# First adaLN modulation of a diffusion trunk: a four-row product with split weights, or feature tiles with row sums on VectorE

## The chip, the cores and the metric

One core of one Trainium2 chip runs the whole program. The metric is the device time of one execution in microseconds (us), shown as the median of several runs.

## The reference, cut to what matters

Two layers work on 512 latent tokens and 256 context tokens of 1024 features. Ahead of each sub-layer the tokens are normalised, scaled and shifted; scale and shift come from the conditioning vectors `c` and `c_ctx` through `w_mod`. The change touches this for the first sub-layer of layer 0, and the product with the key and value columns of `w_in` that follows:

```
silu_c  = silu(c)                                   # (1, 1024); silu_cc likewise from c_ctx
sh1, sc1, g1, sh2, sc2, g2 = split(silu_c @ w_mod[0] + b_mod[0], 6)
h  = rmsnorm(x,  norm1_g[0]) * (1 + sc1)  + sh1     # 512 x 1024
hc = rmsnorm(xc, norm1_g[0]) * (1 + csc1) + csh1    # 256 x 1024
gk, gv = columns of h @ w_in[0] and hc @ w_in[0]    # 768 x 256
```

All inputs are fp32. Products of large size are made from parts: a value is split into `hi`, rounded to the matmul type fp32r, and `lo`, the rest, and three matmuls (hi hi, hi lo, lo hi) are summed.

## The kernel before, in words

Features lie on the 128 partitions, in eight tiles `k`; the 768 tokens are columns. Before layer 0 there is a start section (L407 to L499) in which the order of every engine and of the DMA queue on SP is written out by hand: the string `START` (L40) is a list of codes, each code calls a step, and each step appends its instructions to its engines' queues. The order of the codes is therefore the order in which each engine works, and an engine stops at the first instruction that waits.

The steps of the start section are these.

- `s` (L206) loads a piece of `w_mod`, 128 x 1024, into `sraw`. There are 16, four for each block of 512 output features; the four blocks are shift 0 to 511, scale 0 to 511, then the second halves.
- `e` and `E` (L211) split a piece into `shi` (ScalarE) and `slo` (VectorE for `e`, GpSimd for `E`). Nine of the 16 pieces are split.
- `t` (L219) multiplies a piece: the conditioning vectors are the stationary operand (4 columns), the weights stream through with 512 columns. A piece that was not split streams in fp32.
- `f` and `F` (L229, L233) copy the four rows of a finished block out, turn them onto partitions with four small matmuls, and write `mods` and, for scale, `scl1`.
- `x` (L412) loads a tile of the tokens (128 x 768), squares it and adds it to `acc`. `r` (L421) turns `acc` into `rb`, the reciprocal root for each token on all partitions: matmuls `ss`, `nv` on VectorE, the power `nr` on GpSimd, `dg` on VectorE, matmuls `nbc`, two copies.
- `d` and `p` (L435) multiply a token tile by `rb` on VectorE or GpSimd. `n` (L439) applies scale and shift and writes `hh`. `m` and `M` (L452) write `hl` on VectorE or GpSimd.
- `w` and `W` load and split the key and value weights. `g` (L457) makes the key and value product of four feature tiles: 6 token tiles x 3 matmuls each, into six PSUM tiles `kv0`. It is called with 0 and with 4, each time for four tiles.

After the codes, `silu_rows` (L467) makes `cb`, silu of both conditioning vectors spread over all partitions, with ScalarE and GpSimd. `cb` is what `mods_rest` (L248) needs later: it makes all other modulations as row sums on VectorE (L262), one `scalar_tensor_tensor` with an accumulator for each tile and vector.

The start section's pool is closed behind it. The tile `gt` (L586) lies in memory that the pool gave back, so its load waits until the last user of that memory is done. `rtab` (L596) needs `gt` and `rraw` (L588), and on VectorE it stands ahead of the value copies `gv` (L684), which free the PSUM tiles that the next product (L569) writes.

Of the kernel before, what the change touches and what calls it, by code (L numbers as in the profile page):

```python
# [88 lines left out]
def trunk(es: ExitStack, tc: tile.TileContext, xin, cvec, crow, vecs, gq, rope, wmod_s, wmod_t, w_in, w_gqa,  # L89
# [45 lines left out]

    cs4 = cp.tile([P, KT, 4], F32R, name="cs4")
    dve.tensor_copy(cs4[:, :, 0:2], cs)
    dve.tensor_sub(cs4[:, :, 2:4], cs, f32(cs4[:, :, 0:2]))
    cs0 = cp.tile([P, KT, 4], F32, name="cs0")
    dve.memset(cs0, 0.0)  # L140
    dve.tensor_copy(cs0[:, :, 0:2], cs)
    sel = cp.tile([4, 2], F32, name="sel")
    dve.tensor_add(sel, ident[0:4, 0:2], ident[0:4, 2:4])
# [58 lines left out]
    def mods_start(sp, blk):  # L202

        st = {}

        def load(kk):  # L206
            raw = sp.tile([P, 1024], F32, tag="sraw", bufs=6, name="sraw")
            dma.dma_start(raw, wmod_s[blk, kk])
            st[kk] = [(cs0, raw)]

        def split(kk, eng):  # L211
            raw = st[kk][0][1]
            hi = sp.tile([P, 1024], F32R, tag="shi", bufs=3, name="shi")
            lo = sp.tile([P, 1024], F32R, tag="slo", bufs=3, name="slo")
            act.copy(hi, raw)
            eng.tensor_sub(lo, raw, f32(hi))
            st[kk] = [(cs4, hi), (cs4, lo)]

        def mul(kk):  # L219
            if kk == 0:  # L220
                st["ps"] = psum("mm", "mps")
            for i in range(2):
                k = kk * 2 + i
                n = len(st[kk])
                for j, (c, w) in enumerate(st[kk]):
                    pe.matmul(st["ps"][0:4, :], c[:, k, :], w[:, i * 512:i * 512 + 512],
                              start=k + j == 0, stop=k == KT - 1 and j == n - 1)

        def row():  # L229
            st["row"] = sp.tile([4, 512], F32, tag="srow", bufs=2, name="srow")  # L230
            act.copy(st["row"], st["ps"][0:4, :])

        def fin():  # L233
            po = psum("t", "mpo")
            for i in range(4):
                pe.matmul(po[:, 2 * i:2 * i + 2], st["row"][:, i * P:i * P + P], sel, start=True, stop=True)
            f0 = blk * 4
            dve.tensor_tensor(mods[0][:, f0:f0 + 4, :], po[:, 0:8].rearrange("p (i v) -> p i v", v=2),
                              lv(0, V_BM + f0, 4).unsqueeze(2).broadcast_to([P, 4, 2]), ALU.add)
            if blk >= 2:  # L240
                f = f0 - 8
                for v in range(2):
                    dve.scalar_tensor_tensor(scl1[0][:, f:f + 4, v], mods[0][:, 8 + f:12 + f, v], 1.0,
                                             lv(0, V_N1 + f, 4), ALU.add, ALU.mult)

        return dict(s=load, e=lambda kk: split(kk, dve), E=lambda kk: split(kk, pool), t=mul, f=row, F=fin)
# [160 lines left out]
    with (tc.tile_pool(name="start", bufs=1) as sp,  # L407
# [49 lines left out]
        def kv_part(k0):  # L457

            for k in range(k0, k0 + 4):
                wh, wl = w2_first[k // 4]  # L460
                o = (k % 4) * 256
                for t, ps in enumerate(kv0):
                    for i, (a, w) in enumerate(((H[0][k], wh), (H[0][k], wl), (H[1][k], wh))):
                        pe.matmul(ps[:, :256], a[:, t * P:(t + 1) * P], w[:, o:o + 256],
                                  start=k + i == 0, stop=k == KT - 1 and i == 2)

        def silu_rows():  # L467

            raw = [mp.tile([P, D], F32, tag="mraw", bufs=2, name="crow") for _ in range(2)]
            th = [sp.tile([P, 1024], F32, tag="sraw", bufs=6, name="cth") for _ in range(2)]  # L470
            for v in range(2):
                dma.dma_start(raw[v], crow[v:v + 1, :].broadcast_to([P, D]))
                act.activation(th[v], raw[v], AF.Tanh, scale=0.5)
                pool.tensor_scalar(th[v], th[v], 0.5, 0.5, ALU.mult, ALU.add)
                pool.tensor_mul(cb[:, v, :], th[v], raw[v])

        for q in START.split():
            kind, i = q[0], int(q[1:])
            if kind == "w":
                w2_raw.append(raw_w(w_gqa[0, 2, i], 1024))  # L480
            elif kind == "W":
                w2_first.append(split_w(w2_raw[i], 1024))
            elif kind == "x":
                load_x(i)
            elif kind == "r":
                r_part(i)
            elif kind == "n":
                norm_part(i)
            elif kind in "mM":
                norm_low(i, dve if kind == "m" else pool)  # L490
            elif kind in "dp":
                xr_part(i, dve if kind == "d" else pool)
            elif kind in "fF":
                blks[i][kind]()
            elif kind == "g":
                kv_part(i)
            else:
                blks[i // 4][kind](i % 4)
# [1057 lines left out]
```

## Time and profile before

| what | us |
|---|---|
| median of 3 runs (2310.33 to 2311.14) | 2310.59 |
| the profiled execution | 2311.89 |
| its span, first to last instruction | 2310.1 |
| TensorE busy in the span | 2249.6 |
| VectorE busy | 1451.9 |
| ScalarE busy | 850.1 |
| GpSimd busy | 318.1 |

The profile is of one execution; 1.8 us lie outside its span. Busy time of TensorE counts matmuls from start to modelled end. "Releaser" is what ended an engine's wait. The granted clock of TensorE is given as a share of its upper level: 1.00 is 2.4 GHz and 0.50 is 1.2 GHz.

### The profile page before, as it was taken

How to read it: one execution, taken by the hardware profiler on the slowest of the kernel's cores; microseconds unless marked ns; L12 is line 12 of the kernel's file. 1: busy time of each engine (PE TensorE's matmuls, PEld its weight loads, DVE VectorE, ACT ScalarE, POOL GpSimd, SP SyncE). 2: the span in 40 equal slices, each digit the busy share in tenths (PEclk: the TensorE clock that was granted, in tenths of full speed). 3: DMA queues.
4: the chain of work that ended last, by engine and by line, in shares of the span. 5: the costliest groups of instructions: out<-in, count | busy, mean ns of one | idle time of the engine just before them, and what ended most of it. 6: DMA issues, size and time to landing. Idle time of an engine off the chain costs nothing.

```text
span 2310.1 us, 33414 instructions
## 1 busy us (share of the span) xinstructions
PE 2249.6 (97%) x12895; PEld 1953.2 (85%) x12895; DVE 1451.9 (63%) x2623; ACT 850.1 (37%) x1607; POOL 318.1 (14%) x308
## 2 busy tenths in 40 slices
PE   6899999999999999999999999999999999999998
PEld 2889888999888888888888888888888778888887
DVE  6596978877776366744532358978877655433334
ACT  5324555445621242112112234555445424322223
POOL 4301311112133020000000012311111221000000
PEclk9999999999999999999999999999999999999999
DMA  7432324444355324524521224233343553432322
GB/s 258 128 110 81 106 99 121 135 126 126 128 200 179 93 92 131 162 91 156 166 89 64 68 100 122 87 122 110 114 136 116 173 164 95 147 100 90 102 91 83
DMA packets 98463, 281.06 MB, mean 122 GB/s; under 512 B 12032, under 2 KB 19328, under 8 KB 98304
## 3 DMA queue, kind: packets, MB, share of 16 engines
q1 hardware_dynamic: 98304, 278.92, 38.1%
q8 instruction: 102, 1.67, 0.3%
q14 instruction: 57, 0.47, 0.1%
HBM read 228.15 MB, written 24.51 MB: 109 GB/s over the span
## 4 chain that ended last, share of the span: by engine, by line
PE 65%; DVE 2%; issue 1%; ACT 1%; DMA 0%; POOL 0%; SPq 0%; POOLq 0%; DVEq 0%; ACTq 0%
PE fg L190 13%; PE fu L190 13%; PE fo L190 13%; PE gt L190 6%; PE wo L190 5%; PE br L190 4%; PE o L1047 2%; PE gq L569 2%; PE s L970 2%; PE nv L190 1%; PE nk L190 1%; PE pt L1022 1%; PE nq L190 1%; PE ga L190 1%; PE va L190 1%
## 5 line engine op out<-in xcount | busy, mean ns | idle before, releaser
L172 ACT CAST whi<-wraw 128x1024 fp32r<-128x1024 f32 (+1 forms) x276 | 286.4, 1038 | 623.8 <-PE fo L190 181.8
L173 DVE TENSOR_TENSOR wlo<-wraw,whi 128x1024 fp32r<-128x1024 f32 (+1 forms) x276 | 343.0, 1243 | 215.6 <-ACT whi L172 210.1
L1004 POOL TENSOR_SCALAR pt<-pt,sm 128x768 f32<-128x768 f32 (+1 forms) x160 | 145.2, 907 | 761.8 <-DVE sm L1003 519.3
L752 DVE SCALAR_TENSOR_TENSOR y<-u,vec,y 128x783 f32<-128x783 f32 (+1 forms) x240 | 218.7, 911 | 1.5
L190 PE MATMUL gt<-hh,whi 128*128 128x512 f32 (+1 forms) x576 | 212.4, 369 | 0.0
L190 PE MATMUL gt<-hh,wlo 128*128 128x512 f32 (+1 forms) x576 | 204.8, 356 | 0.0
L190 PE MATMUL gt<-hl,whi 128*128 128x512 f32 (+1 forms) x576 | 204.7, 355 | 0.0
L190 PE MATMUL fo<-hidh,whi 128*128 128x512 f32 (+1 forms) x549 | 192.4, 350 | 0.0
L190 PE MATMUL fo<-hidh,wlo 128*128 128x512 f32 (+1 forms) x549 | 191.7, 349 | 0.0
L190 PE MATMUL fg<-hl,whi 128*128 128x512 f32 (+1 forms) x544 | 190.4, 350 | 1.1 <-POOL hl L342 0.9
L190 PE MATMUL fo<-hidl,whi 128*128 128x512 f32 (+1 forms) x549 | 191.5, 349 | 0.0
L190 PE MATMUL fg<-hh,whi 128*128 128x512 f32 (+1 forms) x544 | 190.3, 350 | 1.1 <-ACT hh L337 1.1
L190 PE MATMUL fg<-hh,wlo 128*128 128x512 f32 (+1 forms) x544 | 189.7, 349 | 0.0
L190 PE MATMUL fu<-hh,whi 128*128 128x512 f32 (+1 forms) x536 | 188.5, 352 | 0.6 <-ACT whi L172 0.6
L190 PE MATMUL fu<-hh,wlo 128*128 128x512 f32 (+1 forms) x536 | 188.3, 352 | 0.8 <-DVE wlo L173 0.8
L190 PE MATMUL fu<-hl,whi 128*128 128x512 f32 (+1 forms) x536 | 188.4, 352 | 0.0
L1024 ACT CAST pTh<-pt 128x384 fp32r<-128x384 f32 (+2 forms) x224 | 104.8, 497 | 136.9 <-PE pt L1022 136.1
L1025 DVE TENSOR_TENSOR pTl<-pt,pTh 128x384 fp32r<-128x384 f32 (+2 forms) x224 | 123.7, 568 | 19.5 <-ACT pTh L1024 18.3
L1365 DVE SCALAR_TENSOR_TENSOR xn<-fo,mods,xn 128x512 f32<-128x512 f32 (+1 forms) x75 | 48.2, 643 | 133.5 <-PE fo L190 133.5
L1348 DVE TENSOR_TENSOR sg<-fu,sg 128x512 f32<-128x512 f32 (+1 forms) x67 | 39.9, 595 | 137.8 <-PE fu L190 137.8
L190 PEld LDWEIGHTS gt<-hh,wlo 128*128 128x128 f32 x576 | 108.7, 189 | 16.3
L190 PEld LDWEIGHTS gt<-hh,whi 128*128 128x128 f32 x576 | 109.0, 189 | 11.1 <-ACT gtan L945 0.3
(264 smaller groups left out, 5449.1 us busy)
## 6 DMA issues: line engine op xcount, KB each, us to landing
wraw<-w_in SPq DMA_DIRECT2D x88, 512.0 KB, 3.5
wraw<-w_fi SPq DMA_DIRECT2D x88, 512.0 KB, 3.3
mraw<-wmod_t SPq DMA_DIRECT2D x80, 512.0 KB, 4.2
wraw<-w_fo SPq DMA_DIRECT2D x32, 448.0 KB, 3.4
gd<-gtan SPq DMA_DIRECT2D x48, 256.0 KB, 2.0
wraw<-w_br SPq DMA_DIRECT2D x24, 512.0 KB, 3.5
tg<-gd SPq DMA_DIRECT2D x24, 384.0 KB, 5.6
sraw<-wmod_s SPq DMA_DIRECT2D x16, 512.0 KB, 5.4
```

The costliest lines, as they stand in the source:

```text
L172: act.copy(hi[:, :n], raw[:, :n])
L173: last_lo[0] = dve.tensor_sub(lo[:, :n], raw[:, :n], f32(hi[:, :n])).ins
L190: pe.matmul(ps[:, :c1 - c0], w[:, k, :], a[k][:, c0:c1], start=i == 0, stop=i == 3 * n - 1)
L569: pe.matmul(ps[:, :256], a[k][:, t * P:(t + 1) * P], w[:, o:o + 256], start=i == 0, stop=i == 3 * KT - 1)
L752: dve.scalar_tensor_tensor(y[:, :YW], u[:, t:t + YW], w, y[:, :YW], ALU.mult, ALU.add)
L970: pe.matmul(o, Q[:, qc], k, start=i == 0, stop=i == 1)
L1004: pool.tensor_scalar(pt[:, :w], pt[:, :w], sm[:, 3:4], 1.0, ALU.mult, ALU.mult)
L1024: act.copy(hv[:, qi, k0:k0 + step, :], pv)
L1025: dve.tensor_tensor(lw[:, qi, k0:k0 + step, :], pv, f32(hv[:, qi, k0:k0 + step, :]), ALU.subtract)
L1047: pe.matmul(ops[:, o:o + n], v.rearrange("p z d -> p (z d)"), m, start=i == 0, stop=i == len(seq) - 1)
L1348: dve.tensor_mul(sg[:, c0:c1], ps[:, :c1 - c0], sg[:, c0:c1])
L1365: dve.scalar_tensor_tensor(XT[f][:, c0:c1], mrg["pf", f, c0][:, :c1 - c0], mods[l][:, 40 + f, v:v + 1], XT[f][:, c0:c1], ALU.mult, ALU.add)
```

## The change

The modulation is made in tiles of 128 features instead of blocks of 512, and three ways stand beside each other in a new `START`.

- `a` and `A`, `S`: the eight scale tiles. The weight tile is loaded in feature order, is the stationary operand in fp32, unsplit, and the two conditioning vectors stream through as two columns; eight matmuls make one tile. `S` adds the bias and makes `scl1`.
- `b` and `B`, `T`: the same for shift tiles 0 to 2.
- `c` and `C`: shift tiles 3 to 7 are row sums on VectorE, two `scalar_tensor_tensor` of 128 x 1024 for each tile, with the rows of `w_mod` transposed.
- `k`: `cb` is made at the start. The two silu vectors, which lie across partitions, are written to DRAM (`crow`) element by element and read back spread over all partitions. `silu_rows` and its work on ScalarE and GpSimd are gone.
- `g` is now one feature tile, and stands behind the `n` and `m` of that tile.

The splits of the modulation weights, the row copies and the turning matmuls are gone.

```diff
 START = (
-    "s0 s1 E1 E0 t0 t1 s2 x0 x1 x2 t2 x3 x4 x5 x6 x7 r0 s3 s4 e4 r1 s5 e5 t3 s8 E8 s7 f0 e7 s6 s10 t4 r2 "
-    "F0 d0 d4 d6 t5 t6 d2 t7 p1 p7 s11 f1 t8 F1 E11 n0 d3 s9 t9 n1 s12 m0 s13 w0 s15 t10 s14 e13 t11 f2 "
-    "W0 t12 M1 w1 e15 t13 W1 p5 t14 t15 f3 F2 n2 M2 F3 n3 n4 n5 n6 m3 M4 n7 m6 M7 g0 m5 g4")
+    "a0 x0 k0 x1 x2 x3 a1 k1 x4 x5 x6 x7 b0 b1 a2 b2 w0 a3 c3 a4 c4 w1 a5 c5 a6 c6 a7 c7 "
+    "A0 S0 A1 S1 r0 B0 T0 B1 T1 r1 A2 S2 B2 T2 r2 d0 n0 M0 W0 d1 n1 m1 A3 S3 g0 p2 n2 M2 C3 g1 A4 S4 d3 n3 m3 "
+    "g2 p4 C4 A5 S5 n4 M4 g3 W1 A6 S6 d5 C5 n5 m5 g4 p6 C6 A7 S7 n6 M6 g5 C7 d7 n7 m7 g6 g7")
...
-    def mods_start(sp, blk):
...
+    def row_sum(raw, v, last, dst):
+
+        o = raw if last else mp.tile([P, D], F32, tag="mprod", bufs=1, name="mprod")
+        dve.scalar_tensor_tensor(o, raw, 1.0, cb[:, v, :], ALU.mult, ALU.mult, accum_out=dst)
...
+        def load_mod(kind, k):
+            raw = raws[kind, k] = sp.tile([P, D], F32, tag="srow" if kind == "c" else "sraw",
+                                          bufs=3 if kind == "c" else 8, name="sraw")
+            f = 8 + k if kind == "a" else k
+            dma.dma_start(raw, wmod_t[0, f] if kind == "c" else wmod_s[f])
+
+        def mul_mod(kind, k):
+
+            ps = sums[kind, k] = psum("t", "mps")
+            raw = raws[kind, k]
+            for kt in range(KT):
+                pe.matmul(ps[:, 0:2], raw[:, kt * P:(kt + 1) * P], cs[:, kt, :], start=kt == 0, stop=kt == KT - 1)
+
+        def row_mod(k):
+            s = sums["b", k] = small("ms", 8)
+            for v in range(2):
+                row_sum(raws["c", k], v, v == 1, s[:, v:v + 1])
+
+        def end_mod(kind, k):
+            f = 8 + k if kind == "a" else k
+            dve.tensor_tensor(mods[0][:, f, :], sums[kind, k][:, 0:2],
+                              lv(0, V_BM + f).broadcast_to([P, 2]), ALU.add)
+            if kind == "a":
+                dve.scalar_tensor_tensor(scl1[0][:, k, :], mods[0][:, f, :], 1.0,
+                                         lv(0, V_N1 + k).broadcast_to([P, 2]), ALU.add, ALU.mult)
+
+        def vec_rows(i):
+
+            if i == 0:
+                for v in range(2):
+                    dma.dma_start(crow[v].rearrange("k p -> p k"), cs[:, :, v])
+            else:
+                for v in range(2):
+                    dma.dma_start(cb[:, v, :], crow[v:v + 1].rearrange("v k p -> v (k p)").broadcast_to([P, D]))
...
-        def kv_part(k0):
+        def kv_part(k):
 
-            for k in range(k0, k0 + 4):
-                wh, wl = w2_first[k // 4]
...
+            wh, wl = w2_first[k // 4]
+            o = (k % 4) * 256
+            for t, ps in enumerate(kv0):
+                for i, (a, w) in enumerate(((H[0][k], wh), (H[0][k], wl), (H[1][k], wh))):
+                    pe.matmul(ps[:, :256], a[:, t * P:(t + 1) * P], w[:, o:o + 256],
+                              start=k + i == 0, stop=k == KT - 1 and i == 2)
...
-        def silu_rows():
...
-        silu_rows()
```

Three places show how the order moves. The first is SP's DMA queue from the first piece of `w_mod` to the last token tile. Before (`sraw` is a piece of `w_mod`, `x_...` a token tile):

```order
L208 DMA sraw<-wmod_s 128x1024 x3
L416 DMA x_143<-xin 128x768
L416 DMA x_146<-xin 128x768
L416 DMA x_151<-xin 128x768
L416 DMA x_158<-xin 128x768
L416 DMA x_163<-xin 128x768
L416 DMA x_168<-xin 128x768
L416 DMA x_173<-xin 128x768
L416 DMA x_178<-xin 128x768
L208 DMA sraw<-wmod_s 128x1024 x11
```

With the change, behind the load of `a0` and of the first token tile (`mraw` belongs to a modulation of later use; its load moves up because nothing else holds its buffer now):

```order
L209 DMA mraw<-wmod_t 128x1024
L393 DMA crow<-cs 128x8x1 x2
L400 DMA x_120<-xin 128x768
L209 DMA mraw<-wmod_t 128x1024
L400 DMA x_125<-xin 128x768
L400 DMA x_130<-xin 128x768
L367 DMA sraw<-wmod_s 128x1024
L396 DMA cb<-crow 128x1024 x2
L400 DMA x_139<-xin 128x768
L400 DMA x_144<-xin 128x768
L400 DMA x_149<-xin 128x768
L400 DMA x_154<-xin 128x768
```

Ahead of the last token tile there are now six loads of 512 KB that are not tokens, where there were three, and two writes of `crow`.

The second place is TensorE around the sums of squares (`ss`) and the spread of the reciprocal root (`nbc`). Before (`mps` is the modulation):

```order
L281 MATMUL ss<-ones,acc 128x1 x6
L226 MATMUL mps<-sraw,cs_87 4x512 x2
L226 MATMUL mps<-shi,cs_84 4x512
L226 MATMUL mps<-slo,cs_84 4x512
L226 MATMUL mps<-shi,cs_84 4x512
L226 MATMUL mps<-slo,cs_84 4x512
L303 MATMUL nbc<-dg,ones 128x512
L303 MATMUL nbc<-dg,ones 128x256
```

With the change, up to the first key product (`gq`):

```order
L374 MATMUL mps<-cs,sraw 128x2 x16
L230 MATMUL ss<-ones,acc 128x1 x6
L374 MATMUL mps<-cs,sraw 128x2 x32
L252 MATMUL nbc<-dg,ones 128x512
L252 MATMUL nbc<-dg,ones 128x256
L374 MATMUL mps<-cs,sraw 128x2 x8
L447 MATMUL gq<-whi,hh 128x256
```

Four modulation tiles (32 matmuls) now stand between `ss` and the spread `nbc`; and on VectorE `dg`, which `nbc` needs, stands behind the additions of the first two of them.

The third place is VectorE in the middle of the start section. Before (`xr`: `d` and `n`, `hl`: `m`, `slo` and `wlo`: splits):

```order
L445 TENSOR_SCALAR xr<-xr,scl_0_94,mods_92 128x512
L437 TENSOR_TENSOR xr<-x_158,rb 128x768
L445 TENSOR_SCALAR xr<-xr,scl_0_94,mods_92 128x512
L453 TENSOR_TENSOR hl<-xr,hh 128x768
L216 TENSOR_TENSOR slo<-sraw,shi 128x1024
L173 TENSOR_TENSOR wlo<-wraw,whi 128x1024
L216 TENSOR_TENSOR slo<-sraw,shi 128x1024
L173 TENSOR_TENSOR wlo<-wraw,whi 128x1024
```

With the change, around feature tiles 3 and 4 (`mprod` and `sraw`: row sums):

```order
L421 TENSOR_TENSOR xr<-x_130,rb 128x768
L429 TENSOR_SCALAR xr<-xr,scl_0_86,mods_84 128x512
L437 TENSOR_TENSOR hl<-xr,hh 128x768
L197 SCALAR_TENSOR_TENSOR mprod,ms<-sraw,cb 128x1024
L197 SCALAR_TENSOR_TENSOR sraw,ms<-sraw,cb 128x1024
L383 TENSOR_TENSOR mods_84<-ms,vec 128x2
L383 TENSOR_TENSOR mods_84<-mps,vec 128x2
L386 SCALAR_TENSOR_TENSOR scl_0_86<-mods_84,vec 128x2
L429 TENSOR_SCALAR xr<-xr,scl_0_86,mods_84 128x512
L165 TENSOR_TENSOR wlo<-wraw,whi 128x1024
```

The pairs of row sums stand between the norms of the feature tiles, five pairs in all; of the splits `slo`, two on VectorE and one on GpSimd stood behind `rb` before. The rows of every engine behind the start section are as before.

## Rows read from the trace of the kernel before

**Rows 1.** Busy time by stretch of 10 us: engines, granted clock, DMA share, GB/s.

```profile
10.00:20.00 10.00, 5.56 (x12) 1.02 (x11) 7.72 (x7) 7.32 (x9) 3.33 (x2) 1.00 1.03 408
...
40.00:50.00 10.00, 7.35 (x20) 1.22 (x18) 8.85 (x9) 7.03 (x9) 4.89 (x3) 1.00 0.64 212
...
100.00:110.00 10.00, 10.00 (x57) 8.74 (x56) 7.26 (x13) 1.82 (x3) 2.79 (x10) 1.00 0.69 159
```

**Rows 2.** Timeline, 0 to 32 us: start, duration, engine, line, tiles, what ended the wait.

```profile
11.65 8.87 DVE L317 TENSOR_TENSOR acc<-acc,sq 128x768 f32<-128x768 f32 x7 [6.43 <-ACT sq L316]
...
14.71 2.79 ACT L316 ACTIVATE sq<-x 128x768 f32<-128x768 f32 x3 [0.16 <-DMA x<-xin]
...
20.58 1.50 PE L281 MATMUL ss<-ones,acc 128*128 128x1 f32 x12 [1.81 <-DVE acc L317]
...
22.36 2.27 POOL L288 TENSOR_TENSOR nr<-nv,mhalf 128x6 f32<-128x6 f32 x1 [9.03 <-DVE nv L286]
...
27.81 2.93 PE L303 MATMUL nbc<-dg,ones 128*128 128x512 f32 x4 [2.91 <-DVE dg L293]
...
30.77 0.37 ACT L430 COPY rb<-nbc 128x256 f32<-128x256 f32 x1 [0.27 <-PE nbc L303]
```

**Rows 3.** DMA issues by line: size, median us from issue to landing.

```profile
cT<-cvec SPq DMA_DIRECT2D x1, 8.0 KB, 1.6
```

**Rows 4.** Timeline of VectorE and GpSimd, 43 to 49 us, where both want to work.

```profile
43.34 1.82 POOL L453 TENSOR_TENSOR hl<-xr,hh 128x768 fp32r<-128x768 f32 x1 [3.04 <-ACT hh L448]
...
44.24 2.00 DVE L216 TENSOR_TENSOR slo<-sraw,shi 128x1024 fp32r<-128x1024 f32 x1 [1.15 <-ACT shi L215]
...
45.11 2.82 POOL L437 TENSOR_TENSOR xr<-x,rb 128x768 f32<-128x768 f32 x1
...
46.17 2.85 DVE L173 TENSOR_TENSOR wlo<-wraw,whi 128x1024 fp32r<-128x1024 f32 x1
```

**Rows 5.** Timeline, 40 to 53 us, instructions that nothing holds up.

```profile
40.82 0.95 DVE L437 TENSOR_TENSOR xr<-x,rb 128x768 f32<-128x768 f32 x1
...
41.69 0.54 DVE L445 TENSOR_SCALAR xr<-xr,scl,mods 128x512 f32<-128x512 f32 x1
...
42.15 0.95 DVE L453 TENSOR_TENSOR hl<-xr,hh 128x768 fp32r<-128x768 f32 x1
...
42.43 0.83 ACT L448 CAST hh<-xr 128x768 fp32r<-128x768 f32 x1
...
48.94 1.22 DVE L216 TENSOR_TENSOR slo<-sraw,shi 128x1024 fp32r<-128x1024 f32 x1
...
52.97 0.17 DVE L238 TENSOR_TENSOR mods<-mpo,vec 128x8 f32<-128x8 f32 x1 [0.28 <-PE mpo L236]
```

**Rows 6.** Instructions of tile `mprod`, the later row sums: duration ns min/median/max.

```profile
L262 DVE SCALAR_TENSOR_TENSOR mprod<-mraw,cb x48: 1205/1218/1753, 97.4 to 1037.1; 128x1024 f32<-128x1024 f32 x48
```

**Rows 7.** Timeline, 61 to 78 us, the end of the start section.

```profile
61.84 2.39 POOL L453 TENSOR_TENSOR hl<-xr,hh 128x768 fp32r<-128x768 f32 x1 [1.34 <-issue]
...
69.70 2.36 POOL L475 TENSOR_TENSOR cb<-cth,crow 128x1024 f32<-128x1024 f32 x1
...
70.12 0.28 PE L464 MATMUL gq<-whi,hl 128*128 128x256 f32 x1
...
72.09 0.33 SPq L586 DMA_DIRECT2D gt<-gq  x1
...
74.39 1.96 DVE L596 SCALAR_TENSOR_TENSOR rtab<-rraw,gt 128x384 f32<-128x384 f32 x4 [8.06 <-DMA gt<-gq]
...
76.60 0.58 PE L569 MATMUL gq<-whi,hh 128*128 128x256 f32 x1 [6.21 <-DVE gv L684]
```

**Rows 8.** Tile `rraw`: its DMA's time from issue to landing.

```profile
DMA to landing us min/median/max: 3.0/3.6/4.1
```

**Rows 9.** Busy time by stretch of 1 us, columns as in rows 1.

```profile
79.00:80.00 1.00, 1.00 (x7) 1.00 (x7) 1.00 (x8) 0.00 (x0) 0.91 (x1) 0.50 0.00 0
...
83.00:84.00 1.00, 1.00 (x11) 1.00 (x10) 0.79 (x3) 0.00 (x0) 0.00 (x0) 1.00 0.25 78
```

More of the change, by code (lines that the diff above doesn't have):

```diff
@@ L88, in trunk @@
 @with_exitstack
-def trunk(es: ExitStack, tc: tile.TileContext, xin, cvec, crow, vecs, gq, rope, wmod_s, wmod_t, w_in, w_gqa,
+def trunk(es: ExitStack, tc: tile.TileContext, xin, cvec, vecs, gq, rope, wmod_s, wmod_t, w_in, w_gqa,
           rpb, w_br, w_out, w_fi, w_fo, out):
@@ L134, in trunk @@
     dve.tensor_mul(cs, cth, cT)
[L136 to L143, printed above, removed]
     mods = [cp.tile([P, 48, 2], F32, name="mods%d" % l) for l in range(DEPTH)]
@@ L147, in trunk @@
     cb = cp.tile([P, 2, D], F32, name="cb")
+    crow = dp.tile([2, KT, P], F32, name="crow")
     hlb = cp.tile([P, DEPTH * 4], F32, name="hlb")
@@ L199, in group @@
         drain(group_steps(*args))
-    def mods_start(sp, blk):
[L204 to L246, printed above, removed]
+    def row_sum(raw, v, last, dst):
+        o = raw if last else mp.tile([P, D], F32, tag="mprod", bufs=1, name="mprod")
+        dve.scalar_tensor_tensor(o, raw, 1.0, cb[:, v, :], ALU.mult, ALU.mult, accum_out=dst)
     def mods_rest(l, blk, nv=2):
@@ L258, in piece @@
                 dma.dma_start(raw, wmod_t[l, f0 + i])
-            raw = st["raw"]
-            o = raw if v == nv - 1 else mp.tile([P, D], F32, tag="mprod", bufs=1, name="mprod")
             c = v * 4 + i
-            dve.scalar_tensor_tensor(o, raw, 1.0, cb[:, v, :], ALU.mult, ALU.mult, accum_out=st["s"][:, c:c + 1])
+            row_sum(st["raw"], v, v == nv - 1, st["s"][:, c:c + 1])
         def fin():
@@ L411, in trunk @@
         xts = []
-        blks = [mods_start(sp, blk) for blk in (0, 2, 1, 3)]
+        raws, sums = {}, {}
+        def load_mod(kind, k):
[26 more added lines that the diff above has]
+                    dma.dma_start(cb[:, v, :], crow[v:v + 1].rearrange("v k p -> v (k p)").broadcast_to([P, D]))
         def load_x(f):
@@ L455, in trunk @@
         kv0 = [psum(q, "gq") for q in ("mm", "s", "s", "mm", "mm", "o")]
-        def kv_part(k0):
-            for k in range(k0, k0 + 4):
-                wh, wl = w2_first[k // 4]
[L461 to L465, printed above, removed]
@@ L467, in silu_rows @@
-        def silu_rows():
[L469 to L475, printed above, removed]
@@ L477, in trunk @@
-        for q in START.split():
[L478 to L498, printed above, removed]
@@ L499, in trunk @@
-        silu_rows()
+        def kv_part(k):
[5 more added lines that the diff above has]
+                              start=k + i == 0, stop=k == KT - 1 and i == 2)
+        steps = dict(x=load_x, k=vec_rows, r=r_part, n=norm_part, g=kv_part, C=row_mod,
+                     w=lambda i: w2_raw.append(raw_w(w_gqa[0, 2, i], 1024)),
+                     W=lambda i: w2_first.append(split_w(w2_raw[i], 1024)),
+                     A=lambda i: mul_mod("a", i), B=lambda i: mul_mod("b", i),
+                     S=lambda i: end_mod("a", i), T=lambda i: end_mod("b", i),
+                     m=lambda i: norm_low(i, dve), M=lambda i: norm_low(i, pool),
+                     d=lambda i: xr_part(i, dve), p=lambda i: xr_part(i, pool))
@@ L501, in trunk @@
+        for kind in "abc":
+            steps[kind] = lambda i, kind=kind: load_mod(kind, i)
+        for q in START.split():
+            steps[q[0]](int(q[1:]))
+            if q[0] == "C":
+                end_mod("b", int(q[1:]))
     for l in range(DEPTH):
@@ L1506, in ftiles @@
         return w.reshape(L, KT, P, n, P).transpose(0, 3, 2, 1, 4).reshape(L, n, P, KT * P)
+    wm = a["w_mod"]
+    d["wmod_s"] = c(ftiles(wm[:, :, :2048])[0])
+    d["wmod_t"] = c(wm.transpose(0, 2, 1).reshape(L, 48, P, D))
     w = a["w_in"]
```

4 lines of the change are left out of this document (removed).

## Prediction

> **What bounds the kernel now.** I read the busy time by stretch first. From 100 us on TensorE is busy 10.00 of 10 us at granted clock 1.00 [rows 1], and the change moves no instruction behind the start section. So whatever time TensorE takes up the next product (L569) earlier or later reaches the end one to one. Before the change that is at 76.60 [rows 7]. I then read the timeline of the start section to see what sets this moment, in four steps.
>
> (1) The reciprocal root: the token tiles arrive at 408 GB/s, a queue that is full [rows 1]; the last square ends at 14.71 + 2.79 = 17.50, `acc` at 20.52, `ss` starts at 20.58, `nbc` at 27.81, and the last copy of `rb` ends at 31.14 [rows 2].
>
> (2) The norms, from `rb` to the last `hl`, which GpSimd ends at 61.84 + 2.39 = 64.23 [rows 7]: 33.1 us. Here VectorE and GpSimd do not work at the same time. GpSimd's `hl` takes 1.82 us when it starts at 43.34, and ends at 45.16; VectorE's split begins at 44.24 and takes 2.00, against 1.22 when nothing holds it up; GpSimd's next begins at 45.11 and takes 2.82; VectorE's next begins at 46.17 and takes 2.85 [rows 4, 5]. Each looks like its own duration plus the rest of the other engine's. So I add up the two engines' work. Before, that is on VectorE 5 x 0.95 (`d`) + 8 x 0.54 (`n`) + 4 x 0.95 (`m`) + 5 x 1.22 (three `wlo` and two `slo`) and some 1.5 of small ones, 20.5 [rows 5]; on GpSimd 7 x 1.82 and one split of 2.3, 15.0. The sum, 35.5, is close to the 33.1 that it took: the pair of engines bounds this step.
>
> (3) TensorE is then done with the key product at 70.12 + 0.28 = 70.40. (4) It waits 6.2 us: GpSimd's last `cb` ends at 72.06, `gt` is issued at 72.09, `rtab` starts at 74.39, the first `gv` frees a PSUM tile, and L569 starts at 76.60 [rows 7].
>
> **The change, part by part.**
>
> *Tokens.* Six loads of 512 KB stand ahead of the last token tile instead of three: 1.57 MB more, at 408 GB/s [rows 1] 3.9 us. The two writes of `crow` in single elements have no like in the trace. They cost nothing at best, if they pass beside the rest; the nearest row is `cT`, 128 short runs that land in 1.6 us [rows 3], and 1024 runs each would be 12.8 us by proportion, 25.6 for the two. I take 2.0, since most of `cT`'s 1.6 is a fixed delay that more runs do not multiply. The Trainium skill (DMA: Bandwidth & Descriptors, Rules for kernel authors and Bandwidth) says that a last dimension which is not contiguous becomes one descriptor per element, and gives about 10.5 ns per packet; with 64 on each of 16 engines my estimate by that page is 0.7 us a write, 1.3 for the two, and the time would be 2323.9; no row here shows it. The reading back of `cb` is two of the six loads. Against this stands 2.0 us: `acc` ended 3.0 us behind the last square, because GpSimd's splits slowed VectorE (8.87 for 7 additions, 1.27 each [rows 2]); these splits are gone and one addition of 0.95 is left. Sum: `ss` later by 3.9 + 2.0 - 2.0 = 3.9.
>
> *Spread.* A modulation tile is eight fp32 matmuls with two columns. The nearest row is `ss`, of the same shape with one column: 12 passes for 6 matmuls in 1.50 [rows 2], so 16 passes are 2.0 us. Between `ss` and `nbc` there are now four tiles: 1.5 + 4 x 2.0 = 9.5 us, where it took 7.2 from `ss` to `nbc`. The power on GpSimd (2.27 [rows 2]) and `dg` hide behind them, though `dg` also waits for two of the tiles. 2.3 later. From `nbc` to `rb` I keep 3.3. So `rb` is complete at 31.14 + 3.9 + 2.3 = 37.3. The splits, ScalarE's row copies and the turning matmuls that are gone stood beside these steps or in the pair's sum of the next, and give nothing further.
>
> *The pair of engines.* VectorE from `rb` to the last `m`: 5 x 0.95 + 8 x 0.54 + 4 x 0.95 + 4 x 1.22 = 17.8 [rows 5], ten row sums at 1.22 = 12.2 [rows 6], fifteen additions and scales at 0.17 = 2.5 [rows 5]; 32.5. GpSimd: four `hl` and three `xr`, 7 x 1.82 = 12.7 [rows 4]. In turn that is 45.2. Besides, the `m` of tiles 1, 3, 5 and 7 stand directly behind their `n` and wait for ScalarE's `hh`, 0.83 and the passing on of signals, some 1.1 each: 4.4, or nothing where GpSimd fills the time. I take 4.4, since GpSimd is mostly done by then. So the last `m` ends at 37.3 + 45.2 + 4.4 = 86.9, against 64.23. TensorE has eight products of 18 x 0.12 = 2.2 us in this time and five modulation tiles of 2.0, 27 of 50 us: it is covered by the pair.
>
> *The tail.* The last user of the start pool's memory is now the last row sum. Behind it stand an addition, `d`, `n`, the wait and `m` of tile 7, 0.17 + 0.95 + 0.54 + 1.1 + 0.95 = 3.7: it ends at 83.2, and `gt` goes out then. `rraw` now stands behind `gt` and two bias loads: some 1.4 us of issuing, and 3.0 to 4.1 to land [rows 8], 88.4. From the start of `rtab` to L569 it was 76.60 - 74.39 = 2.2 [rows 7], so L569 starts at 90.6. The eighth key product needs 2 us behind the last `m`, 89, and is hidden by this. The tail shrinks from 12.4 us (64.23 to 76.60) to 3.7: the work of `silu_rows` on GpSimd, which held `gt` up, is gone.
>
> *Clock.* Before, the clock fell in the wait: 7 matmuls in the stretch from 79 at 0.50, 11 at 1.00 in that from 83 [rows 9], about 2.5 us lost over the 5 to 6 us at the lower level. The wait at the end is now short, so up to 2.5 may come back; but TensorE now stands idle some us between the key products, and a last product at 1.2 GHz costs 2 more. I take 0, with both ends kept.
>
> **Sum.** 90.6 - 76.6 = 14.0 us later. The profiled execution took 2311.9 and would take 2325.9; the median of the runs lies 1.3 under it, so I forecast **2324.6** against 2310.6. About 0.2%, 4.6 us, is what a measurement of this kernel tells from no change. Ends of the unknown costs: `crow` 2 less, waits 4.4 less, clock 2.5 less gives +5.1; `crow` 6 more and clock 2 more gives +22. The forecast's own range is 2317 to 2332.
>
> **Rivals.**
>
> (A) *Not slower: the two engines overlap in the row sums.* GpSimd's seven instructions then lie beside VectorE's row sums, which have gaps or accesses that differ from those of a split. For it: no row shows a row sum with an accumulator beside a GpSimd `hl`; the longest took 1753 ns against 1205 [rows 6], a stretch of half a us and not of 1.82. Against it: rows 4, and all that GpSimd meets is not row sums. At 12.7 us less, and the clock's 2.5, it is 14.0 - 15.2 = -1.2, 2309.4. It decides at the wait that each GpSimd instruction adds: under 0.83 of its 1.82 us, the result lies within 0.2%, and if tokens also come earlier it is faster. Chance 0.15.
>
> (B) *The element writes block the queue.* Behind `crow` stand the token tiles x1 to x7 on the same queue. If its 1024 runs cost 6 us a write instead of 1 (half of what `cT` gives by proportion), everything is 10 us later: 2334.6. For it: SP issues nothing of `cb` until `crow` is written. Chance 0.10.
>
> (C) *TensorE becomes the bound at the lower clock.* With idle times between products the clock can stay at 1.2 GHz; eight products of 3.8 and five tiles of 4.0 are then 50 us, as long as the pair's, and the waits add up instead of hiding: some 6 us more, 2330.6. Against it: between 40 and 50 us TensorE was busy for 7.35 of 10 us and kept 1.00 [rows 1]. Chance 0.10.
>
> **How the numbers follow.** The forecast has 0.65, A 0.15, B 0.10, C 0.10. Faster by over 0.2% (under 2306.0) needs A together with early tokens: 0.06. Within 0.2% is the rest of A and the lowest end of the forecast: 0.13. Slower: 0.81. The range of 8 in 10 takes in part of A and of B: 2311 to 2336.
>
> **What would show it.** In the changed profile: `ss` starts near 24.5 and `nbc` near 34; `rb` at 37; VectorE and GpSimd together busy in nearly all of 38 to 87, with stretched instructions on both; the last `hl` near 87 and L569's successor near 91, with `rtab` waiting for `rraw`; behind that the same rows as before, shifted. The forecast is wrong if `rb` is ready before 34, if row sums show 1.2 us while GpSimd works beside them, or if the next product starts before 82.

## The result and the profile after

The changed kernel takes 2337.97 us (median of 4 runs, 2335.05 to 2339.12) against 2310.86 for the kernel before on the same chip (4 runs): ratio 1.0109, 95% interval 1.0088 to 1.0129, 27.1 us slower. The forecast was 14.0 us slower and a range up to 2336. The profiled execution took 2339.12 us with a span of 2337.3.

The next product (L532 now, L569 before) starts at 104.74 us instead of 76.60, 28.1 later, and behind it the order of the work is as before. The loss is thus in the first 105 us. Busy time there, by stretch of 10 us (columns: engines PE, PEld, DVE, ACT, POOL; granted clock, DMA share, GB/s):

```profile
10.00:20.00 10.00, 0.00 (x0) 0.00 (x0) 0.73 (x1) 0.84 (x1) 0.00 (x0) 1.00 0.85 140
20.00:30.00 10.00, 3.57 (x16) 3.49 (x16) 4.78 (x6) 4.99 (x6) 0.00 (x0) 1.00 1.03 415
30.00:40.00 10.00, 8.58 (x41) 8.58 (x41) 1.98 (x8) 0.07 (x1) 1.35 (x1) 1.00 1.03 410
40.00:50.00 10.00, 10.00 (x41) 8.88 (x42) 1.51 (x5) 0.25 (x1) 0.00 (x0) 1.00 0.51 202
...
80.00:90.00 10.00, 6.46 (x38) 6.08 (x37) 8.94 (x14) 2.48 (x3) 0.29 (x1) 0.67 0.45 150
90.00:100.00 10.00, 7.12 (x34) 6.03 (x34) 8.08 (x14) 2.87 (x4) 1.80 (x1) 0.67 0.31 97
```

From 10 to 20 us the DMA engines are 0.85 busy and move 140 GB/s, where it was 408 [rows 1]; no engine computes before 18 us. The two writes of `crow` (the first line has their issue, the second their size and the median time from issue to landing), and three of the stretches of 1 us while they run, with the first behind them:

```profile
L393 SPq DMA_DIRECT2D crow<-cs x2: 390/486/583, 5.2 to 5.7; - x2
...
crow<-cs SPq DMA_DIRECT2D x2, 4.0 KB, 10.8
```

```profile
8.00:9.00 1.00, 1.00 (x7) 1.00 (x6) 0.00 (x0) 0.00 (x0) 0.00 (x0) 1.00 1.16 4
...
11.00:12.00 1.00, 0.00 (x0) 0.00 (x0) 0.00 (x0) 0.00 (x0) 0.00 (x0) 1.00 1.02 65
...
14.00:15.00 1.00, 0.00 (x0) 0.00 (x0) 0.00 (x0) 0.00 (x0) 0.00 (x0) 1.00 1.01 43
...
17.00:18.00 1.00, 0.00 (x0) 0.00 (x0) 0.00 (x0) 0.00 (x0) 0.00 (x0) 1.00 0.91 311
```

The writes carry 8 KB in all. While they run the DMA engines are busy with little to show for it: from 11 to 12 us their share is 1.02 at 65 GB/s. Over all nine stretches from 8 to 17 us the share lies between 0.20 and 1.16, 0.77 in the mean, and no stretch moves more than 96 GB/s. In the microsecond from 17 the queue is back at 311. The first square of a token tile shows what that does to the tokens:

```profile
18.39 0.84 ACT L265 ACTIVATE sq<-x 128x768 f32<-128x768 f32 x1 [10.40 <-DMA x<-xin]
```

Its tile was issued at 6.30, right behind the writes. SP's issue of `cb`, which has to wait for the writes, comes only at 15.87, so that wait is not what delayed this tile.

Then comes the reciprocal root with its spread, to be read beside [rows 2] (timeline, 28 to 55 us):

```profile
31.42 2.72 PE L230 MATMUL ss<-ones,acc 128*128 128x1 f32 x12 [4.99 <-DVE mods L383]
...
34.01 13.79 PE L374 MATMUL mps<-cs,sraw 128*128 128x2 f32 x64
...
47.66 2.91 PE L252 MATMUL nbc<-dg,ones 128*128 128x512 f32 x4
...
50.60 0.37 ACT L414 COPY rb<-nbc 128x256 f32<-128x256 f32 x1 [0.27 <-PE nbc L252]
```

`ss` comes 10.8 us later than before, and its 12 passes take 2.72 where they took 1.50. The four modulation tiles are 64 passes in 13.79 us, 0.215 each, 3.4 us a tile. `rb` is complete at 50.97. The same form has another price later in this trace, behind key products (timeline, 60 to 108 us):

```profile
65.07 1.88 PE L374 MATMUL mps<-cs,sraw 128*128 128x2 f32 x16
```

That is 0.118 a pass.

VectorE and GpSimd in the norms, 62 to 68 us, to be read beside [rows 4]:

```profile
62.07 1.22 DVE L197 SCALAR_TENSOR_TENSOR mprod<-sraw,cb 128x1024 f32<-128x1024 f32 x1
...
63.15 1.83 POOL L437 TENSOR_TENSOR hl<-xr,hh 128x768 fp32r<-128x768 f32 x1 [5.03 <-ACT hh L432]
...
63.33 2.74 DVE L197 SCALAR_TENSOR_TENSOR sraw<-sraw,cb 128x1024 f32<-128x1024 f32 x1
64.93 2.81 POOL L421 TENSOR_TENSOR xr<-x,rb 128x768 f32<-128x768 f32 x1
...
66.11 1.65 DVE L383 TENSOR_TENSOR mods<-ms,vec 128x2 f32<-128x2 f32 x1
```

A row sum alone takes 1.22. The next one starts 0.18 behind a GpSimd `hl` and takes 2.74, so it ends 1.09 after `hl` does (64.98): nearly all of its own work lies behind `hl`. GpSimd's `xr`, begun while that row sum runs, takes 2.81; even the addition of 128 x 2 behind it takes 1.65 instead of 0.16: it ends at 67.76, and `xr` at 67.74. Last, the end of the start section, beside [rows 7]:

```profile
95.72 0.33 SPq L549 DMA_DIRECT2D gt<-gq  x1
...
98.25 0.96 DVE L437 TENSOR_TENSOR hl<-xr,hh 128x768 fp32r<-128x768 f32 x1 [0.95 <-ACT hh L432]
...
101.11 1.96 DVE L559 SCALAR_TENSOR_TENSOR rtab<-rraw,gt 128x384 f32<-128x384 f32 x4 [1.90 <-DMA rraw<-rope]
102.98 1.04 ACT L164 CAST whi<-wraw 128x1024 fp32r<-128x1024 f32 x1 [4.76 <-PE gq L447]
...
104.39 1.64 DVE L647 TENSOR_TENSOR gv<-gq,gv 128x128 fp32r<-128x128 f32 x5 [1.31 <-ACT gv L646]
...
104.74 0.38 PE L532 MATMUL gq<-whi,hh 128*128 128x256 f32 x1 [1.79 <-DVE gv L647]
```

The last `hl` ends at 99.21, the next product starts 5.5 us later. `rtab` waits for `rraw`, as forecast; but it is done at 103.07. What came last is ScalarE's `whi`, done at 104.02, which waited for the eighth key product; ScalarE's first copy of `gv`, for which VectorE's waits, stands behind it. The matmuls of that key product run at the lower pace, 0.21 each, and end at 102.94.

### The profile page after: what moved, and what is told of

Same layout as the page of the kernel before. It is cut to its first block, busy times and chain, and to the rows that moved or that the text cites. A ratio compares the mean times of both kernels' runs of the same rounds, so it can differ in the third digit from the quotient of the medians.

```text
span 2337.3 us, 33561 instructions
## 1 busy us (share of the span) xinstructions
PE 2266.8 (97%) x12975; PEld 1987.6 (85%) x12975; DVE 1455.9 (62%) x2649; ACT 837.7 (36%) x1592; POOL 300.4 (13%) x300
## 4 chain that ended last, share of the span: by engine, by line
PE 64%; DVE 2%; DMA 1%; ACT 1%; issue 1%; POOL 0%; SPq 0%; POOLq 0%; DVEq 0%; ACTq 0%
PE fg L182 13%; PE fu L182 13%; PE fo L182 13%; PE gt L182 5%; PE wo L182 4%; PE br L182 4%; PE o L1010 2%; PE gq L532 2%; PE s L933 1%; PE nv L182 1%; PE nk L182 1%; PE pt L985 1%; PE nq L182 1%; PE ga L182 1%; PE va L182 1%
## 5 line engine op out<-in xcount | busy, mean ns | idle before, releaser
L182 PEld LDWEIGHTS gt<-hh,wlo 128*128 128x128 f32 x576 | 108.7, 189 | 16.2
```

The source lines that it names most:

```text
L182: pe.matmul(ps[:, :c1 - c0], w[:, k, :], a[k][:, c0:c1], start=i == 0, stop=i == 3 * n - 1)
```

## The experiments

Each kernel is the changed kernel with the edit shown, but for the last, which is an edit of the kernel before. The table has where the chain stands in each profile (start of `ss`, of `nbc`, end of the last copy of `rb`, end of the last `hl`, start of the next product; us), and the median time. The kernel before stood at 2310.12 to 2311.01 beside them.

| run | `ss` | `nbc` | `rb` | last `hl` | next product | time |
|---|---|---|---|---|---|---|
| before | 20.58 | 27.81 | 31.14 | 64.23 | 76.60 | 2310.86 |
| after | 31.42 | 47.66 | 50.97 | 99.21 | 104.74 | 2337.97 |
| e1_no_element_writes | 22.68 | 38.91 | 42.23 | 90.46 | 95.76 | 2329.84 |
| e2_no_gpsimd | 32.23 | 48.47 | 51.79 | 97.40 | 102.93 | 2340.19 |
| e3_all_on_pe | 20.41 | 36.65 | 39.96 | 98.04 | 104.28 | 2336.21 |
| e4_spread_first | 33.15 | 38.55 | 41.88 | 103.24 | 107.42 | 2341.40 |
| e5_products_ahead | 33.36 | 44.74 | 48.05 | 96.28 | 101.76 | 2334.58 |
| e6_rows_transposed | 23.28 | 39.51 | 42.83 | 91.05 | 96.19 | 2328.77 |
| e7_rows_transposed_products_between | 25.29 | 46.26 | 49.07 | 97.33 | 101.34 | 2334.91 |
| e8_no_row_sums | 23.57 | 39.81 | 43.12 | 79.45 | 83.47 | 2318.40 |
| e9_no_row_sums_short_tiles | 23.68 | 29.07 | 32.41 | 69.48 | 74.83 | 2307.57 |
| b1_before_tanh_tiles_apart | 20.55 | 27.80 | 29.83 | 63.50 | 71.01 | 2305.51 |

The median times follow the next product within 3 us. The rest of the span moves that much from run to run, so these stations are the sharper reading; the two runs of e3 alone lie 9.3 us apart.

### e1: no element writes

`crow` is an input that holds the rows, and only the reads of `cb` are left (the silu of these rows is left out).

```diff
-                for v in range(2):
-                    dma.dma_start(crow[v].rearrange("k p -> p k"), cs[:, :, v])
...
```

> The change, with `cb` read from an input that holds the two conditioning rows instead of from `crow`; the two element writes are gone. It leaves out the silu of these rows, so the row sums have other values; the work per instruction is the same. Theory (the element writes hold up the DMA queue: 9 us at about 50 GB/s behind them): `ss` starts 9 us earlier, 31.4 to 22.5, everything behind shifts with it, L532 from 104.7 to about 96, the time from 2338 to 2329. Rival (it is the three more loads of 512 KB that hold up the tokens, 3.9 us of the 10.8): `ss` at most 2 us earlier, time 2336.

Ratio 1.0083 [1.0054, 1.0112]. `ss` starts 8.7 us earlier and all that follows moves with it, as the theory had it. The writes cost 8.7 us, not 2.0. What is left, `ss` 2.1 later than before, is what the forecast has for tokens without its `crow` term, 1.9.

### e2: no GpSimd in the norms

In `START` every `M` becomes `m` and every `p` becomes `d`: VectorE does GpSimd's seven instructions.

```diff
-    ... d0 n0 M0 W0 ... p2 n2 M2 ... p4 ... n4 M4 ... p6 ... n6 M6 ...
+    ... d0 n0 m0 W0 ... d2 n2 m2 ... d4 ... n4 m4 ... d6 ... n6 m6 ...
```

> The change, with the seven GpSimd instructions of the norms (`M` and `p`) moved to VectorE in the same places (`m` and `d`). Theory (VectorE and GpSimd take turns, so each GpSimd instruction costs VectorE its whole 1.82 us): the stretch from `rb` to the last `hl`, 48.2 us, loses 7 x (1.82 - 0.95) = 6.1 us and gains up to 4 x 1.1 us of waits for ScalarE, so 42 to 46.5; time 2332 to 2336. Rival (they overlap, and VectorE alone is the bound): 7 x 0.95 = 6.6 us more, 55 us, time 2345.

Ratio 1.0128 [1.0099, 1.0157]. From `rb` to the last `hl` it takes 45.6 us instead of 48.2, in the theory's range. That stretch, after and in e2 (columns as above; 39.96 and 37.28 are VectorE's busy time):

```profile
51.01:99.21 48.20, 37.65 (x205) 34.81 (x205) 39.96 (x56) 15.25 (x20) 15.54 (x7) 0.82 0.29 91
...
51.79:97.40 45.61, 35.81 (x206) 33.48 (x205) 37.28 (x63) 15.35 (x20) 0.00 (x0) 0.81 0.30 96
```

VectorE alone, with seven instructions more, is busy for less time than beside GpSimd. So the second engine gains nothing here. The next product is 1.8 us earlier, but the time is 2.2 longer and misses the theory's 2332 to 2336; what lengthened the rest of the span was not followed up.

### e3: all tiles on TensorE

Shift tiles 3 to 7 go by `b`, `B`, `T` instead of `c`, `C`, and `k0 k1` move behind `w1`.

```diff
-    ... c3 a4 c4 w1 a5 c5 a6 c6 a7 c7 ... M2 C3 g1 ... C4 ... C5 ... C6 ... C7 ...
+    ... b3 a4 b4 w1 k0 k1 a5 b5 a6 b6 a7 b7 ... M2 B3 T3 g1 ... B4 T4 ... B5 T5 ... B6 T6 ... B7 T7 ...
```

> The change, with shift tiles 3 to 7 made like the first three, on TensorE, instead of as row sums, and the two steps `k` behind the loads of `w1`, behind the tokens. Theory (turns of VectorE and GpSimd bound the norms; the element writes hold up the tokens): `ss` 9 us earlier, and ten row sums, 12.2 us, and their additions leave VectorE, so `rb` to the last `hl` takes 36 us instead of 48.2, unless TensorE with its five more tiles at 3.4 us bounds it; time 2318 to 2322. Rival (TensorE at the lower clock bounds the norms): the five tiles of 3.4 us are added, 17 us, against the 12.2, no gain in that stretch: 2329 or more.

Ratio 1.0111 [1.0062, 1.0159]. The rival's case happened, not the theory's. `ss` is 11 us earlier with `crow` out of the way, but from `rb` to the last `hl` it takes 58.1 us instead of 48.2, which uses up nearly all of that. The stretches say why (columns as above):

```profile
50.00:60.00 10.00, 10.00 (x48) 10.00 (x49) 1.29 (x6) 0.83 (x1) 3.60 (x2) 1.00 0.93 379
60.00:70.00 10.00, 10.00 (x48) 10.00 (x49) 2.83 (x6) 2.04 (x3) 0.00 (x0) 1.00 0.01 2
```

TensorE is busy all of the time and makes 48 matmuls in 10 us, 0.21 each: it bounds this stretch, at the lower pace. VectorE works 4.1 of these 20 us. For the last five tiles TensorE is no better a place than VectorE.

### e4: the spread ahead of the four tiles

```diff
-    ... r0 B0 T0 B1 T1 r1 A2 S2 B2 T2 r2 d0 ...
+    ... r0 r1 r2 B0 T0 B1 T1 A2 S2 B2 T2 d0 ...
```

> The change, with the spread of the root (`r1`, `r2`) moved ahead of the modulation tiles B0, B1, A2, B2 in the order. Theory (TensorE's four tiles at 3.4 us each between `ss` and `nbc` are on the path): `rb` is ready 10 us earlier behind `ss` (9 instead of 19.5 us), the first norm follows one tile later at some 43 to 44 us instead of 52.0; part of this is lost again where later tiles wait on TensorE, so the last `hl` comes 3 to 9 us earlier; time 2329 to 2335. Rival (VectorE's and GpSimd's turns alone count, and the tiles only move): 2338.

Ratio 1.0133 [1.0104, 1.0163]. `rb` is complete 8.7 us behind `ss` instead of 19.6, but `d0` starts only at 55.04: on VectorE it stands behind the additions of the four tiles, which TensorE makes from 41.3 to 55. The tiles stay on the path on either side of the spread, and nothing is gained. The theory missed: the last `hl` is 4.0 us later than in the changed kernel, 1.7 of it already at `ss`, and the time is 3.4 us above the rival's as well.

### e5: wide products ahead of the row norm

```diff
+        def warm(n):
+            for _ in range(n):
+                pe.matmul(kv0[0], ones, xts[5][:, 0:512], start=True, stop=True)
...
-    ... A0 S0 A1 S1 r0 ...
+    ... A0 S0 A1 S1 z4 r0 ...
```

> The changed kernel with four fp32 products of 128x128 by 128x512 (ones by the sixth x tile, into a PSUM tile that is written afresh later) queued on TensorE ahead of the twelve row-norm products. They take 16 passes of 0.43 us at most, 6.9 us, while the last x tiles land and ss is not yet due. In the changed kernel a modulation tile took 3.4 us (52 passes of 0.216 in 11.2 us) where tiles that came after real products took 1.9 (16 passes of 0.118). Theory: the tiles are slow only because TensorE comes to them from idle; with products ahead of them the passes take 0.118, ss to nbc falls from 16.2 to about 9.5 us, and the time is near 2331. Rival: two-column passes do not keep the faster pace, whatever ran ahead of them: after the first few the passes fall back to 0.216, ss to nbc stays at 14 to 16 us, and the time stays at 2337 to 2339.

Ratio 1.0099 [1.0080, 1.0117]. Theory and rival were each half right: `ss` to `nbc` takes 11.4 us instead of 16.2. The stretches show a pace that comes and goes (columns as above; PE's count stands in brackets, the granted clock is the third number from the right):

```profile
35.00:36.00 1.00, 1.00 (x11) 1.00 (x11) 0.00 (x0) 0.00 (x0) 0.96 (x1) 1.00 1.01 401
36.00:38.00 2.00, 2.00 (x20) 2.00 (x20) 0.16 (x1) 0.00 (x0) 0.39 (x1) 1.00 1.04 414
38.00:40.00 2.00, 2.00 (x13) 2.00 (x14) 1.03 (x2) 0.00 (x0) 0.00 (x0) 0.63 1.02 408
40.00:42.00 2.00, 2.00 (x11) 2.00 (x11) 0.32 (x2) 0.00 (x0) 0.00 (x0) 0.50 1.03 401
42.00:44.00 2.00, 2.00 (x11) 2.00 (x11) 0.00 (x0) 0.00 (x0) 0.00 (x0) 0.50 1.03 412
```

Behind the wide products the passes run at 1.00, 2.4 GHz, 20 in a stretch of 2 us (a pass that only reaches into a stretch is counted too). Then, with TensorE busy 2.00 of 2.00 and nothing but two-column passes on it, the granted clock falls to 0.50, 1.2 GHz, and a stretch of 2 us has 11. The two-column passes did not hold the upper level here.

### e6: the rows written from a transposed copy

```diff
-                for v in range(2):
-                    dma.dma_start(crow[v].rearrange("k p -> p k"), cs[:, :, v])
+                ps = psum("t", "cps")
+                pe.matmul(ps[0:16, 0:P], cs.rearrange("p k v -> p (k v)"), ident, start=True, stop=True)
+                ct = sp.tile([P, P], F32, tag="ct", bufs=1, name="ct")
+                dve.tensor_copy(ct[0:16, :], ps[0:16, 0:P])
+                dma.dma_start(crow, ct[0:16, :])
...
```

`crow` now holds the 16 rows in the order of the transposed copy, and the two reads of `cb` follow it.

> The changed kernel with the two conditioning rows written to DRAM from a transposed copy: one product with the identity, one PSUM copy, and one write of 16 runs of 512 bytes instead of two writes of 1024 runs of 4 bytes each. What is computed is the same. Theory (the 4-byte runs hold the DMA engines for some 9 us): ss comes at 22 to 24 us instead of 31.4, as in the run without writes (22.7), and the time is 2329 to 2331. Rival (a write and a read of DRAM that depend on each other hold the queue, whatever the runs): ss stays at 29 to 32 and the time at 2336 to 2339.

Ratio 1.0074 [1.0055, 1.0092]; `ss` at 23.28 as the theory had it, and 9.2 us less than the changed kernel. The same 8 KB, in 16 runs of 512 bytes, leave the queue at 387 GB/s:

```profile
10.00:20.00 10.00, 3.54 (x16) 3.49 (x16) 3.83 (x4) 4.21 (x5) 0.00 (x0) 1.00 1.05 387
```

And the chain on TensorE, where only the start has moved (timeline, 8 to 62 us):

```profile
23.28 2.72 PE L230 MATMUL ss<-ones,acc 128*128 128x1 f32 x12 [5.37 <-DVE mods L383]
25.86 13.79 PE L374 MATMUL mps<-cs,sraw 128*128 128x2 f32 x64
39.51 2.91 PE L252 MATMUL nbc<-dg,ones 128*128 128x512 f32 x4
```

The pages count the packets, after and in e6:

```profile
DMA packets 100543, 281.07 MB, mean 120 GB/s; under 512 B 14112, under 2 KB 21408, under 8 KB 100384
...
DMA packets 100287, 281.07 MB, mean 121 GB/s; under 512 B 12048, under 2 KB 21408, under 8 KB 100128
```

The kernel before has 12032 under 512 bytes, so the two writes bring 2080, one for each of the 2048 elements and 32 more; e6 brings 16. It is the 4-byte runs that cost, not the write and the read that depends on it. Spread over 16 engines, 8.7 us for 2048 elements is some 68 ns an element on its engine, an estimate from e1.

### e7: wide products between the tiles, on top of e6

```diff
-    ... S1 r0 B0 T0 B1 T1 r1 A2 S2 B2 T2 r2 ...
+    ... S1 z4 r0 B0 z1 T0 B1 z1 T1 r1 A2 z1 S2 B2 z1 T2 r2 ...
```

> The transposed write of the conditioning rows, the four products ahead of the row norm, and one more product of 128x128 by 128x512 behind each of the four modulation tiles that stand between row norm and broadcast. If wide products bring and keep the faster pace, tiles take 1.9 us each, ss at 22 to 24 is followed by nbc some 10.5 us later, and the time is 2322 to 2325. If they don't, each of the four products adds 1.7 us to the chain, ss to nbc is 18 to 22 us, and the time is 2331 to 2336.

Ratio 1.0100 [1.0082, 1.0119]: 6.1 us more than e6, as the second case had it. One wide product behind each tile does not bring the faster pace back (timeline, 8 to 62 us):

```profile
26.55 2.64 PE L374 MATMUL mps<-cs,sraw 128*128 128x2 f32 x16
29.05 2.06 PE L456 MATMUL gq<-x,ones 128*128 128x512 f32 x2
30.90 3.41 PE L374 MATMUL mps<-cs,sraw 128*128 128x2 f32 x16
```

The granted clock is 0.50 from 28 to 48 us; it is back at 0.99 from 48 to 50, behind the last wide product and `nbc`.

### e8: no row sums, on top of e6

```diff
-            for v in range(2):
-                row_sum(raws["c", k], v, v == 1, s[:, v:v + 1])
+            dve.memset(s[:, 0:2], 0.0)
```

> The transposed write of the conditioning rows, and the ten row sums of the shift tiles 3 to 7 left out: zeros stand in their place, so that these five modulation tiles hold only their bias; their raw tiles and the broadcast of the rows are still loaded. Taken away are ten VectorE operations of 1.2 to 1.75 us, 12 to 17 us of the 48 in which VectorE and GpSimd stand between rb and the last hl. Theory (the stretch is the sum of what VectorE and GpSimd do, since they hinder each other): rb to the last hl falls from 48 to 32 to 36 us, and the time from 2328.8 to 2314 to 2318. Rival (TensorE bounds the stretch as well: 144 key products at the slower pace of 0.213 are 30.7 us, five modulation tiles at 1.9 to 3.4 another 9.5 to 17): the last key product stays 40 to 48 us behind rb, and the time is 2322 to 2328.

Ratio 1.0038 [1.0024, 1.0052], 10.4 us less than e6. `rb` to the last `hl` is 36.3 us instead of 48.2: 11.9 less, and ten row sums of 1.22 are 12.2. They add to the stretch one to one. The last key product ends 38.6 us behind `rb`, under the 40 to 48 of the rival, and the time is 0.4 us above the theory's upper edge.

### e9: short tiles as well, on top of e8

```diff
-            for kt in range(KT):
+            nk = 1 if (kind, k) in (("b", 0), ("b", 1), ("a", 2), ("b", 2)) else KT
+            for kt in range(nk):
...
```

> As the run without row sums, and the four modulation tiles between row norm and broadcast take one pass of eight each (the other seven eighths of their sums are left out). Theory (these tiles are on the path with 3.4 us each): ss to nbc falls from 16.2 to 4 to 6 us, and the time by another 9 to 11 us, to 2304 to 2308 if the row sums gave 12, which is the time of the kernel before: the three parts (4-byte writes, tiles ahead of the broadcast, row sums in the norm) are then the whole of the loss. Rival (something behind the norm holds the end, the tail or TensorE): less than 6 us beside the run without row sums, 2310 or more.

Ratio 0.9988 [0.9977, 0.9999], 10.8 us less than e8. The four tiles are now eight passes, and the spread follows (timeline, 20 to 36 us):

```profile
26.25 1.85 PE L375 MATMUL mps<-cs,sraw 128*128 128x2 f32 x8
29.07 2.93 PE L252 MATMUL nbc<-dg,ones 128*128 128x512 f32 x4 [0.97 <-DVE dg L242]
```

With the 4-byte writes, the row sums and seven eighths of these tiles taken out, the new order is at the time of the kernel before, or 3 us under it. The three parts are 9.2, 10.4 and 10.8 us by the medians. That they add up to 30.4, the way from 2337.97 to 2307.57, shows nothing by itself, as each run builds on the one above it; what counts is that each part is of the size expected for it. And this run leaves out work that the kernel before does, so it is no measure of a new order that computes everything.

### b1: the kernel before, with the tanh scratch in another pool

```diff
-            th = [sp.tile([P, 1024], F32, tag="sraw", bufs=6, name="cth") for _ in range(2)]
+            th = [mp.tile([P, 1024], F32, tag="mprod", bufs=1, name="cth") for _ in range(2)]
```

> The kernel before with one edit: the two scratch tiles of the tanh come from the pool of the modulation's products instead of the pool that the start section's tiles come from, so that the memory of gt, the next raw tile and the rope table no longer waits for GpSimd's last pass over the conditioning rows. The results are the same. Theory (the 12.4 us tail before the next product is a wait for that memory: gt issued at 72.09 behind the cb pass that ends at 72.06): gt and raw tiles are issued some 6 us earlier, the next product stands at about 70.8 instead of 76.6, and the time is 2302 to 2306, below both kernels. Rival (something else holds the transfers or the product, the key products' end or the rope table): 2 us or less is gained, 2308 to 2311.

2305.51 us (9 runs, 2302.99 to 2309.91), ratio 0.9977 [0.9968, 0.9987]: 3.0 to 7.4 us below the kernel before, and 32 below the changed one. `gt` goes out at 52.29 instead of 72.09 [rows 7], 20 us earlier where 6 were expected (timelines, 50 to 75 us, and TensorE's, 69 to 72):

```profile
52.29 0.33 SPq L586 DMA_DIRECT2D gt<-gq  x1
...
65.51 5.01 DVE L596 SCALAR_TENSOR_TENSOR rtab<-rraw,gt 128x384 f32<-128x384 f32 x4
```

```profile
70.89 0.28 PE L464 MATMUL gq<-whi,hl 128*128 128x256 f32 x1
71.01 0.28 PE L569 MATMUL gq<-whi,hh 128*128 128x256 f32 x1
```

The next product follows the last key product without a gap, where TensorE had waited 6.2 us. Of the 5.6 us by which it is earlier, 0.7 stands already at the last `hl`; the rest is the tail. `rtab` now stands beside GpSimd's `cb` and takes 5.01 instead of 1.96, without being waited for.

## Why the prediction was wrong in size

The direction and the place were right: the start section alone, and the next product as the measure of it. None of the three signs of being wrong that the prediction names was seen; all three look for too short a time. Step by step, forecast against the trace of after:

- **Tokens** (`ss` 3.9 later; measured 10.8). This is the first step that failed, in its `crow` term: "I take 2.0, since most of `cT`'s 1.6 is a fixed delay that more runs do not multiply." Without the writes (e1) `ss` is 8.7 earlier. The cost does go by the number of runs (e6), as in the proportion to `cT` that was set aside, at a third of its 25.6. Rival B, with 12 us for the two writes, was the case that happened, at 8.7; that its 2334.6 comes within 3.4 us of the time is luck, since the second step failed as well. The Trainium skill (DMA: Bandwidth & Descriptors, Rules for kernel authors) says that such a pattern becomes one descriptor per element, and the count of packets agrees (2080 more). The estimate of 1.3 us by its price per packet (Bandwidth) is too low by a factor of six to seven; the page has that price from loads issued by GpSimd, and these are writes from SP.
- **Spread** (9.5 us from `ss` to `nbc`; measured 16.2). The second step that failed: "16 passes are 2.0 us", taken from `ss` of [rows 2]. The shape was right and the pace was not. In the kernel before, wide products ran until 1.8 us ahead of `ss`, and a pass took 0.12; in the changed kernel nothing but two-column passes stands ahead of and behind it, and a pass took 0.215. The four tiles took 13.8 us where 8.0 were counted. e5 shows both paces in one stretch, and e9 that these tiles are on the path with all they take.
- **The pair of engines** (49.6 us from `rb` to the last `m`; measured 48.2). Right, and for the stated reason: row sums wait for GpSimd (2.74 for 1.22), e8 finds their 12.2 us as 11.9, e2 finds no gain from having two engines. Rival A, overlap, is out. But the sum is nearer than its terms. VectorE is idle for 8.2 of the 48.2 us: four waits of 0.95 for `hh`, 3.8 where 4.4 were taken, and two of 1.90 for ScalarE's `whi`, which the forecast has at nothing. The instructions that meet GpSimd take some 9.2 us more than when nothing holds them up (an estimate from seven such rows), where 12.7 were counted. That the last two misses offset each other is luck.
- **The tail** (3.7 us; measured 5.5). "The eighth key product needs 2 us behind the last `m`, and is hidden": it took 3.7 at the lower pace and came last. In e7 and e8, where the clock was up, it took 2.2 and the whole tail 4.0.
- **Clock** (0 taken, 2 more as the bad end). Part of what failed in the spread and the tail lies here: TensorE stood at the lower pace for the tiles, and the granted clock is 0.67 from 80 to 100 us. Rival C had the pace right and the place wrong. The lower pace lengthened the spread and the tail; in the norms of this kernel VectorE waits for `hh` and `whi` and never for TensorE, and only in e3 did TensorE bound that stretch.

The misses beyond the forecast, by stations: +6.9 (tokens), +6.7 (spread), -1.4 (norms) and +1.8 (tail), together 14.1 before rounding, which with 14.0 makes the 28.1 of the next product. Two terms, both prices of operations that the trace before did not show in that form, make nearly all of it.

That e9 is slightly under the time of before can be read from the stations: its tail is 5.4 us instead of 12.4, which more than makes up for 1.3 at `rb` and 4.0 in the norms. What stays open is why the clock falls under two-column passes. That the tiles of the changed kernel ran at 1.2 GHz is inferred from the time of a pass, as the record of the clock does not show it there.
